# Strassen-Winograd MLP, mixers and experts on one core: a plain first block, one load of small parameters, another split of the convolutions' weights, and unread products

## The chip, the core and the metric

The kernel runs on one core of a Trainium2 chip. The core has five engines that follow their own instruction queues in order and wait for each other through semaphores: TensorE (PE in the profile; PEld is its weight load), VectorE (DVE), ScalarE (ACT), GpSimd (POOL) and SyncE (SP, which issues most DMA transfers). The metric is the device time of one execution in microseconds; of several runs the median counts, and less is better.

## The reference

One sequence of 512 tokens with 1024 features goes through two layers of a first kind and one of a second, all in float32. Cut to what matters here:

```python
# layers 0 and 1
p = x @ w_in[l]                                     # split into the mixers' inputs
y = concat(mla(...), mlstm(...), ssd(conv(s_xbc)))  # conv: 5 taps per channel, bias, silu
x = layernorm(alpha * x + y @ w_out[l])
x = layernorm(alpha * x + moe(x))                   # 4 groups of 4 experts, top 2, width 256
# third layer
x = x + mixer2(x) @ w_out_2                         # gated delta net and a linear recurrence
h = rmsnorm(x, norm_mlp_w_2) @ w_ff1_2              # 1024 -> 4096
x = rmsnorm(x + relu(h) ** 2 @ w_ff2_2, final_norm_w_2)
```

## The kernel before, in words

**Numbers.** A float32 operand of a product is held as a pair, h (rounded by a cast, L134) and l (the difference, L139); `split` makes both, with the engines that it is given, and `mm` (L124, L125, L126) adds three products, h·h, l·h and h·l. So each weight costs one cast and one subtraction of 128 x 1024 elements per half megabyte, and TensorE three passes.

**Weights.** `plan` lists all weights in the order of use as tasks; `take`, `done` and `pump` load them ahead (`load`, L229: a transfer of 1 MB from SP into one of two raw buffers, then the split into a ring of four). `self.pat` says which engine makes which half: ("act", "dve") at launch, ("act", "pool") after the gates' projection (L520). A raw buffer is free again when its splits are done.

**Order.** The program is written against a tile framework: each tile name has a number of buffers, and a new tile of a name waits for the readers of the old one. A list scheduler sets the order of every engine's instructions at build time from the dependencies and estimated times; the source does not fix it. Within a queue the order is then strict.

**Launch** (`run`, L1996). Four tiles of xT are loaded and split, `params` (L2007) loads nine small arrays for this and the next layer one by one into tiles of their own (L2014), and `mixer_layer` begins with the gates' projection "C", 312 columns for each of four token tiles, evacuated by `evac_c` (L507 to L515).

**Convolution** (`ssd_conv`, L580). For each of six feature blocks: ScalarE copies the projection into xp (L592), VectorE makes the first tap (L594) and four more (L596), ScalarE a tanh (L598), VectorE the product (L600); TensorE transposes four of the blocks (L605). Beside it stand the gates of the mLSTM (L703 to L725) and the next weights' splits.

**Routing** (`route`, before L1213; the mask sums at L1217 to L1220). From the logits LG a chain of small VectorE operations finds the group and the two best experts; `slot_ids` (L1128, L1141) makes the list of tokens for an expert, an indirect gather (L1089) fetches them, TensorE transposes them (L1096) and multiplies.

**Layer end** (`layer`). After the last expert eight indirect gathers (L2147) bring back the two results of each token into Yg, which are weighted and added (L2161, L2168), normalised, and transposed (L369, L371) for the next layer.

**MLP** (`second`, `mlp`). w_ff1_2 is used in eight blocks of 512 columns, w_ff2_2 in eight of 512 rows. The up product of a block, (512 x 1024) by (1024 x 512), is made as 2 x 2 blocks by Winograd's form of Strassen: seven products of half size (24 instructions each) instead of eight, for which VectorE forms four sums of weights (`up_part`, L260 to L264) and four sums of tokens T1 to T4 (`mlp_in`, L1779 to L1786, once). `fin(i)` ends token tile i of the third layer's mixer: the norm (L1333), eight transposes (L1770), copies into X32 (L1771) and splits. Two of block 0's products (B11, B21) are started early as `begun`. `keep` (L1806, L1807) combines the products, squares, and splits into uT; `down` adds the second product into R (L1837).

PSUM is given out by kind ("mm", "tr", "sm", "dn", "ht"), a few banks each.

Of the kernel before, what the change touches and what calls it, by code (L numbers as in the profile page):

```python
# [8 lines left out]
FR = mybir.dt.float32r  # L9
# [3 lines left out]
OP = mybir.AluOpType  # L13
AX = mybir.AxisListType

P = 128
# [54 lines left out]
class Kernel:  # L71
# [57 lines left out]

    def split(self, dst, src, heng="act", leng="dve"):  # L130

        nc = self.nc
        if heng == "act":
            nc.scalar.copy(dst.h, src)  # L134
        elif heng == "pool":
            nc.gpsimd.tensor_scalar(dst.h, src, 1.0, None, op0=OP.mult)
        else:
            nc.vector.tensor_copy(dst.h, src)
        (nc.gpsimd if leng == "pool" else nc.vector).tensor_tensor(dst.l, src, dst.h, op=OP.subtract)  # L139
# [104 lines left out]

    def up_part(self, b, n, u):

        v = self.nc.vector
        if n == 0:
            self.quarters = []
            for j in range(2):  # L250
                raw = self.t(self.raws[self.nraw % len(self.raws)].pool, "raw", [P, 2 * UNIT])
                self.nraw += 1
                at = b * 512 + j * 256
                self.nc.sync.dma_start(raw.rearrange("p (k n) -> p k n", n=256),
                                       self.a["w_ff1_2"][0][:, at:at + 256].rearrange("(k p) n -> p k n", p=P))
                self.quarters += [raw[:, 0:UNIT], raw[:, UNIT:2 * UNIT]]
# [229 lines left out]
    def mixer_layer(self, l):  # L486
# [33 lines left out]
        self.pat = [("act", "pool")]  # L520
# [25 lines left out]
        self.mla_in(l, m, sp, XT)  # L546
        yc = self.ssd_scan(l, sp, m, Z)
# [32 lines left out]
    def ssd_conv(self, l, m, XT):  # L580
# [7 lines left out]
        def evac(f, p):  # L588
# [5 lines left out]
            nc.vector.tensor_scalar(ac, xp[:, 0:S], cw[:, f:f + 1], cw[:, 30 + f:31 + f], op0=OP.mult, op1=OP.add)  # L594
# [567 lines left out]
    def route(self, pool, LG):  # L1162
# [17 lines left out]


# [4 lines left out]
        v.scalar_tensor_tensor(e2, o1, NEG, el, op0=OP.mult, op1=OP.add)  # L1186
        m2, o2 = top("o2", e2)
# [571 lines left out]
    def mlp_in(self, m, i, n, X, X32):  # L1759


        nc, v = self.nc, self.nc.vector
        tk, half = slice(i % 2 * P, i % 2 * P + P), i // 2
        cut = lambda n: HL(X[n].h[:, :, tk], X[n].l[:, :, tk])
        ps = []
        for g in range(2):
            p = self.ps("tr", [P, 4, P])
            for j in range(4):
                f = 4 * g + j
                nc.tensor.transpose(p[:, j, :], n[:, f * P:(f + 1) * P], self.ident)  # L1770
            nc.scalar.copy(X32[g][:, :, i * P:(i + 1) * P], p)  # L1771
            if not half:
                self.split(cut(("B11", "B21")[g]), p)
            ps.append(p)
        if not half:
            return
        (b11, b12), (b21, b22) = [[x[:, :, z + i % 2 * P:z + i % 2 * P + P] for z in (0, 256)] for x in X32]
        t2 = self.t(m, "u2", [P, S], bufs=2).rearrange("p (k t) -> p k t", k=4)
        v.tensor_tensor(b11, b12, b11, op=OP.subtract)  # L1779
        v.tensor_tensor(t2, b22, b11, op=OP.subtract)  # L1780
        self.split(cut("T2"), t2)
        self.split(cut("T1"), b11)
        v.tensor_tensor(b12, b22, b12, op=OP.subtract)
        self.split(cut("T3"), b12)
        self.split(cut("B22"), ps[1])
        v.tensor_tensor(b21, b21, t2, op=OP.subtract)  # L1786
        self.split(cut("T4"), b21)
# [6 lines left out]
    def mlp(self, m, X, R, begun, finish):  # L1794

        nc, v = self.nc, self.nc.vector
        uT = {}

        def up(b):
# [17 lines left out]
            A, C = (product(0, "B11"), product(1, "B21")) if b else begun  # L1817
# [25 lines left out]
        up(0)  # L1843
# [10 lines left out]
    def second(self):  # L1854
        nc, a, v = self.nc, self.a, self.nc.vector
        with ExitStack() as c:
# [17 lines left out]
            X, begun = {}, []  # L1874

            w0 = [self.hl(rp, t, [P, UNIT]) for t in ("T3", "T4")]
            for n in range(2):
                self.up_part(0, n, w0[n])
            for t in ("B11", "B21", "B22", "T1", "T2"):
                X[t] = self.hl(rp, t, [P, 4, 256])  # L1880
# [3 lines left out]
            def fin(i):  # L1884
                n = self.t(rp, "nrm", [P, D], bufs=2)
                if i == 2:
                    for z in range(2):
                        p = self.ps("dn", [P, S])
                        self.up_product(p, self.by_k(w0[z]), X[("B11", "B21")[z]])
                        begun.append(p)  # L1890
                    for t in ("T3", "T4"):
                        X[t] = self.hl(rp, t, [P, 4, 256])
                self.rms(rp, n, R[:, i], g, jk=n)
                self.mlp_in(rp, i, n, X, X32)
# [4 lines left out]
            with ExitStack() as x1:  # L1899
# [11 lines left out]
                self.mlp(rp, X, R, begun, finish)  # L1911

    def plan(self):
# [42 lines left out]
        def up(b):  # L1956
            for n in range(0 if b else 2, 7):
# [12 lines left out]
    def run(self):  # L1970
        nc, a = self.nc, self.a
        with ExitStack() as ctx:
# [13 lines left out]
            with ExitStack() as c2:  # L1986
                xp = self.pool(c2, "x0", bufs=4, side="right")
                self.tasks = self.plan()
                for i in range(NT):
                    xt = self.t(xp, "xt", [P, KD, P])  # L1990
                    nc.sync.dma_start(xt, a["xT"][i])
                    if i == 0:
                        self.consts()
                        self.set_phase("m", [self.raw0], [self.ring0], [("act", "dve")])
# [12 lines left out]
    def params(self, l):  # L2007

        self.par = r = {}
        width = dict(dtb=8, al=8, sgn=256, cw=48, gcol=32, lc=32, gc=16)  # L2010
        at = 0
        for tag, n in ROWS[l]:
            r[tag] = self.t(self.ppool, "gcol" if tag == "lc" else tag, [P, width.get(tag, n)])[:, 0:n]
            self.nc.sync.dma_start(r[tag], self.a[f"small{l}"][:, at:at + n])  # L2014
            at += n

# [9 lines left out]
    def layer(self, l):  # L2026
# [4 lines left out]
        with ExitStack() as c:  # L2031
# [72 lines left out]
            for s in range(16 + 4):  # L2104
# [10 lines left out]
                if s < 16:  # L2115
                    idx = self.slot_ids(mo, PM[:, s, :], 0, "idx")
                    ex[s] = self.expert(mo, [self.part((l, z, s)) for z in "gud"], idx, store(s))
# [31 lines left out]
            self.gate = [Yg[3][0]] * 2  # L2149
            for i in range(NT):  # L2150
# [92 lines left out]
```

## Time and profile before

| | us |
|---|---|
| median of three runs | 1737.26 |
| lowest and highest | 1736.63, 1739.16 |
| profiled execution | 1732.17 |
| its span | 1730.3 |

The profile is of one execution. Its times are in microseconds from the start of the span. An engine's busy time is the time in which it computes or moves data, without waits and without issuing transfers. In a timeline a row is an instruction (x2: two of the same kind in a row) with its start and duration, its engine, line, operation, and out<-in by the program's names; in brackets stand the idle time of the engine before it and what ended that. Durations of matmuls overlap, since they are pipelined: the distance from start to start is what one costs. PEclk is the granted clock of TensorE, as a share of full speed.

### The profile page before, as it was taken

How to read it: one execution, taken by the hardware profiler on the slowest of the kernel's cores; microseconds unless marked ns; L12 is line 12 of the kernel's file. 1: busy time of each engine (PE TensorE's matmuls, PEld its weight loads, DVE VectorE, ACT ScalarE, POOL GpSimd, SP SyncE). 2: the span in 40 equal slices, each digit the busy share in tenths (PEclk: the TensorE clock that was granted, in tenths of full speed). 3: DMA queues.
4: the chain of work that ended last, by engine and by line, in shares of the span. 5: the costliest groups of instructions: out<-in, count | busy, mean ns of one | idle time of the engine just before them, and what ended most of it. 6: DMA issues, size and time to landing. Idle time of an engine off the chain costs nothing. (4 is left out here: it accounts for less than half of the span.)

```text
span 1730.3 us, 29609 instructions
## 1 busy us (share of the span) xinstructions
PE 1561.6 (90%) x11539; PEld 1398.0 (81%) x11539; DVE 1298.5 (75%) x2480; ACT 827.2 (48%) x1422; POOL 561.3 (32%) x464
## 2 busy tenths in 40 slices
PE   7899999699956899997889993999799799999997
PEld 6789899698946789887878972887578698899996
DVE  6847963789957847865689977777776797777774
ACT  4354562278856344551368863555532533333331
POOL 0555332316114555334315202003411143444341
PEclk9999999899987999999989996999999899999999
DMA  5214123499945211123399964432112243333311
GB/s 183 61 59 147 64 103 115 180 363 357 396 166 204 61 59 48 50 86 131 127 346 358 373 239 170 128 98 74 38 52 75 73 127 117 98 98 98 98 62 49
DMA packets 107662, 248.02 MB, mean 143 GB/s; under 512 B 9460, under 2 KB 70776, under 8 KB 95224
## 3 DMA queue, kind: packets, MB, share of 16 engines
q1 hardware_dynamic: 101624, 225.05, 37.4%
q0 software_dynamic: 5888, 20.97, 3.8%
q8 instruction: 94, 1.54, 0.4%
q14 instruction: 56, 0.46, 0.1%
HBM read 218.21 MB, written 27.79 MB: 142 GB/s over the span
## 5 line engine op out<-in xcount | busy, mean ns | idle before, releaser
L134 ACT CAST wh<-raw 128x1024 fp32r<-128x1024 f32 (+3 forms) x375 | 377.5, 1024 | 278.4 <-PE mm L126 70.3
L139 POOL TENSOR_TENSOR wl<-raw,wh 128x1024 fp32r<-128x1024 f32 (+3 forms) x117 | 281.3, 2414 | 474.7 <-ACT wh L134 469.0
L139 DVE TENSOR_TENSOR wl<-raw,wh 128x1024 fp32r<-128x1024 f32 (+2 forms) x258 | 307.2, 1211 | 64.3 <-ACT wh L134 63.4
L124 PE MATMUL mm<-wh,actTh 128*128 128x256 f32 (+2 forms) x640 | 189.5, 297 | 22.2 <-ACT wh L134 7.9
L126 PE MATMUL mm<-wh,actTl 128*128 128x256 f32 (+2 forms) x640 | 185.7, 292 | 2.9 <-POOL actTl L139 2.4
L125 PE MATMUL mm<-wl,actTh 128*128 128x256 f32 (+2 forms) x640 | 185.9, 291 | 0.5 <-DVE wl L139 0.5
L124 PE MATMUL mm<-actTh,wh 128*128 128x512 f32 x368 | 150.5, 409 | 2.4 <-DVE FD L509 0.8
L126 PE MATMUL mm<-actTh,wl 128*128 128x512 f32 x368 | 148.0, 402 | 0.0
L125 PE MATMUL mm<-actTl,wh 128*128 128x512 f32 x368 | 148.0, 402 | 0.0
L124 PEld LDWEIGHTS mm<-wh,actTh 128*128 128x128 f32 x640 | 124.9, 195 | 25.2 <-ACT wh L134 7.9
L126 PEld LDWEIGHTS mm<-wh,actTl 128*128 128x128 f32 x640 | 123.9, 194 | 5.4 <-POOL actTl L139 3.3
L125 PEld LDWEIGHTS mm<-wl,actTh 128*128 128x128 f32 x640 | 124.8, 195 | 1.8 <-DVE wl L139 0.9
L1089 POOL DMA_INDIRECT G<-Xd,idx x32 | 77.9, 2434 | 131.1 <-DVE oh L1138 58.3
L124 PE MATMUL dn<-wh,uTh 128*128 128x512 f32 x256 | 100.9, 395 | 3.1 <-DVE R L1837 3.1
L126 PE MATMUL dn<-wh,uTl 128*128 128x512 f32 x256 | 100.4, 392 | 0.0
L125 PE MATMUL dn<-wl,uTh 128*128 128x512 f32 x256 | 100.1, 391 | 0.1
L124 PEld LDWEIGHTS mm<-actTh,wh 128*128 128x128 f32 x368 | 70.6, 192 | 17.8 <-PE mm L126 2.2
L126 PEld LDWEIGHTS mm<-actTh,wl 128*128 128x128 f32 x368 | 70.9, 193 | 14.4
L125 PEld LDWEIGHTS mm<-actTl,wh 128*128 128x128 f32 x368 | 71.0, 193 | 14.0
L124 PE MATMUL py<-wh,GTh 128*96 128x256 f32 x256 | 73.6, 287 | 1.3 <-ACT wh L134 1.3
L124 PE MATMUL pg<-wh,GTh 128*96 128x256 f32 x256 | 74.3, 290 | 0.0
L125 PE MATMUL py<-wl,GTh 128*96 128x256 f32 x256 | 72.9, 285 | 1.1 <-DVE wl L139 1.1
(781 smaller groups left out, 4308.4 us busy)
## 6 DMA issues: line engine op xcount, KB each, us to landing
raw<-in_expert_w_gate_dram SPq DMA_DIRECT2D x32, 1024.0 KB, 10.4
raw<-in_expert_w_up_dram SPq DMA_DIRECT2D x32, 1024.0 KB, 10.3
raw<-in_expert_w_down_dram SPq DMA_DIRECT2D x32, 1024.0 KB, 10.9
raw<-in_w_ff_dram SPq DMA_DIRECT2D x32, 1024.0 KB, 5.5
raw<-in_w_in_dram SPq DMA_DIRECT2D x27, 1024.0 KB, 5.4
raw<-in_w_out_dram SPq DMA_DIRECT2D x12, 1024.0 KB, 5.2
Yd<-Ye SPq DMA_DIRECT2D x32, 384.0 KB, 6.7
Yd<-zr SPq DMA_DIRECT2D x9, 512.0 KB, 6.4
```

What stands on the lines that cost most here:

```text
L124: mm(out, lhsT.h, rhs.h, start=start, stop=False, **kw)
L125: mm(out, lhsT.h, rhs.l, start=False, stop=False, **kw)
L126: mm(out, lhsT.l, rhs.h, start=False, stop=stop, **kw)
L134: nc.scalar.copy(dst.h, src)
L139: (nc.gpsimd if leng == "pool" else nc.vector).tensor_tensor(dst.l, src, dst.h, op=OP.subtract)
L1089: nc.gpsimd.indirect_dma_start(out=G[:n], out_offset=None, in_=self.Xd, in_offset=bass.IndirectOffsetOnAxis(ap=idx[:n], axis=0))
```

## The change

- `busy(kind, x, n)` is new: n float32 products of a matrix of ones with x into a tile of PSUM that nobody reads. It is called at launch after the constants (14 times, with the ones themselves), in `route` on LG (10) and on e2 (8), after `slot_ids` for the first four experts (4 on LG), and at the layer end on the first 128 columns of each of the eight gathered tiles (3 each).
- `params` makes one tile "par" and one transfer per layer. The tags are slices of it.
- In `ssd_conv` the first tap moves from VectorE to ScalarE (activation Identity with scale and bias). `self.pat` becomes ("act", "pool") only after the convolutions and the inputs of the attention, so the weights of that stretch get both halves from ScalarE and VectorE.
- MLP: block 0 is a plain product (`up_plain`), 192 instructions, with its four weight tiles as they are (`up_block0`, loaded and split before). It runs feature half by feature half within each token half: (f, t) = (0, 0), (1, 0), (0, 1), (1, 1). The token sums move from `mlp_in` to `mlp_sums`, behind the first quarter of block 0's products, and are taken over 256 tokens at a time; their splits go into the memory of block 0's weights: T2 and T1 after the third quarter, T3 and T4 after the fourth. B12, which the seven products do not need, is held in a raw buffer. Results are relu, square and split, without sums.

```diff
@@ -126,6 +126,12 @@
...
             self.nc.tensor.matmul(out, lhsT, rhs, start=start, stop=stop, **kw)
+    def busy(self, kind, x, n):
+        p = self.ps(kind, [P, x.shape[1]])
+        for _ in range(n):
+            self.nc.tensor.matmul(p, self.ones, x, start=True, stop=True)
@@ -242,18 +248,27 @@
...
+    def up_load(self, b):
+        q = []
+        for j in range(2):
+            raw = self.t(self.raws[self.nraw % len(self.raws)].pool, "raw", [P, 2 * UNIT])
+            self.nraw += 1
+            at = b * 512 + j * 256
+            self.nc.sync.dma_start(raw.rearrange("p (k n) -> p k n", n=256),
+                                   self.a["w_ff1_2"][0][:, at:at + 256].rearrange("(k p) n -> p k n", p=P))
+            q += [raw[:, 0:UNIT], raw[:, UNIT:2 * UNIT]]
+        return q
+    def up_block0(self, ws):
+        for n, (q, w) in enumerate(zip(self.up_load(0), ws)):
+            self.split(w, q, "act", ("dve", "pool")[n // 2])
     def up_part(self, b, n, u):
...
         if n == 0:
-            self.quarters = []
-            for j in range(2):
-                raw = self.t(self.raws[self.nraw % len(self.raws)].pool, "raw", [P, 2 * UNIT])
-                self.nraw += 1
-                at = b * 512 + j * 256
-                self.nc.sync.dma_start(raw.rearrange("p (k n) -> p k n", n=256),
-                                       self.a["w_ff1_2"][0][:, at:at + 256].rearrange("(k p) n -> p k n", p=P))
-                self.quarters += [raw[:, 0:UNIT], raw[:, UNIT:2 * UNIT]]
+            self.quarters = self.up_load(b)
         q = self.quarters
         if n == 2:
             q.append(self.t(self.mlpp, "sw", [P, UNIT]))
@@ -517,7 +532,6 @@
...
         self.cT = self.hl(m, "cT", [P, 3, S])
-        self.pat = [("act", "pool")]
@@ -544,6 +558,7 @@
...
         self.mla_in(l, m, sp, XT)
+        self.pat = [("act", "pool")]
         yc = self.ssd_scan(l, sp, m, Z)
         self.sctx.close()
         with ExitStack() as y:
@@ -591,7 +606,7 @@
...
             ac = self.t(m, "ac", [P, S], bufs=2)
-            nc.vector.tensor_scalar(ac, xp[:, 0:S], cw[:, f:f + 1], cw[:, 30 + f:31 + f], op0=OP.mult, op1=OP.add)
+            nc.scalar.activation(ac, xp[:, 0:S], AF.Identity, scale=cw[:, f:f + 1], bias=cw[:, 30 + f:31 + f])
             for k in range(1, 5):
                 nc.vector.scalar_tensor_tensor(ac, xp[:, k:k + S], cw[:, 6 * k + f:6 * k + f + 1], ac, op0=OP.mult, op1=OP.add)
             th = self.t(m, "th", [P, S])
@@ -1178,12 +1193,14 @@
...
+        self.busy("ht", LG.rearrange("p t e -> p (t e)"), 10)
...
         v.scalar_tensor_tensor(e2, o1, NEG, el, op0=OP.mult, op1=OP.add)
+        self.busy("ht", e2.rearrange("p n e -> p (n e)"), 8)
         m2, o2 = top("o2", e2)
         gl = LG[:, :, 0:4]
         gm, og = top("og", gl)
@@ -1756,45 +1773,64 @@
...
-    def mlp_in(self, m, i, n, X, X32):
-        nc, v = self.nc, self.nc.vector
+    def mlp_in(self, i, n, X, X32):
+        nc = self.nc
         tk, half = slice(i % 2 * P, i % 2 * P + P), i // 2
-        cut = lambda n: HL(X[n].h[:, :, tk], X[n].l[:, :, tk])
-        ps = []
         for g in range(2):
             p = self.ps("tr", [P, 4, P])
             for j in range(4):
                 f = 4 * g + j
                 nc.tensor.transpose(p[:, j, :], n[:, f * P:(f + 1) * P], self.ident)
+            x = X[f"B{g + 1}{half + 1}"]
+            self.split(HL(x.h[:, :, tk], x.l[:, :, tk]), p)
             nc.scalar.copy(X32[g][:, :, i * P:(i + 1) * P], p)
-            if not half:
-                self.split(cut(("B11", "B21")[g]), p)
-            ps.append(p)
-        if not half:
-            return
-        (b11, b12), (b21, b22) = [[x[:, :, z + i % 2 * P:z + i % 2 * P + P] for z in (0, 256)] for x in X32]
-        t2 = self.t(m, "u2", [P, S], bufs=2).rearrange("p (k t) -> p k t", k=4)
+    def mlp_sums(self, X, X32):
+        v = self.nc.vector
+        (b11, b12), (b21, b22) = [[x[:, :, z:z + 256] for z in (0, 256)] for x in X32]
         v.tensor_tensor(b11, b12, b11, op=OP.subtract)
-        v.tensor_tensor(t2, b22, b11, op=OP.subtract)
-        self.split(cut("T2"), t2)
-        self.split(cut("T1"), b11)
         v.tensor_tensor(b12, b22, b12, op=OP.subtract)
-        self.split(cut("T3"), b12)
-        self.split(cut("B22"), ps[1])
-        v.tensor_tensor(b21, b21, t2, op=OP.subtract)
-        self.split(cut("T4"), b21)
+        v.tensor_tensor(b22, b22, b11, op=OP.subtract)
+        v.tensor_tensor(b21, b21, b22, op=OP.subtract)
+        return dict(T1=b11, T2=b22, T3=b12, T4=b21)
...
-    def mlp(self, m, X, R, begun, finish):
+    def mlp(self, m, X, X32, w0, R, finish):
...
         uT = {}
+        def up_plain():
+            u_ = self.hl(m, "uT", [P, 4, S], bufs=2)
+            W = [self.by_k(w) for w in w0]
+            C, T = [], {}
+            for f, t in ((0, 0), (1, 0), (0, 1), (1, 1)):
+                p = self.ps("dn", [P, S])
+                for z in range(2):
+                    for k in range(KD):
+                        x = X[f"B{k // 4 + 1}{t + 1}"][:, k % 4]
+                        self.mm(p[:, z * 256:(z + 1) * 256], W[2 * f + k // 4][k % 4][:, z * P:(z + 1) * P], x,
+                                start=k == 0, stop=k == KD - 1)
+                C.append((f, t, p))
+                if (f, t) == (0, 0):
+                    T = self.mlp_sums(X, X32)
+                for n in {(0, 1): ("T2", "T1"), (1, 1): ("T3", "T4")}.get((f, t), ()):
+                    X[n] = self.hl(m, n, [P, 4, 256])
+                    self.split(X[n], T[n])
+            for f, t, p in C:
+                r, u = self.t(m, "nrm", [P, D], bufs=2)[:, 0:S], self.t(m, "u2", [P, S], bufs=2)
+                nc.scalar.activation(r, p, AF.Relu)
+                v.tensor_tensor(u, r, r, op=OP.mult)
+                self.split(HL(*(x[:, 2 * f:2 * f + 2, 256 * t:256 * t + 256] for x in (u_.h, u_.l))),
+                           u.rearrange("p (f t) -> p f t", f=2), "act")
+            uT[0] = u_
@@ -1814,7 +1850,7 @@
...
-            A, C = (product(0, "B11"), product(1, "B21")) if b else begun
+            A, C = product(0, "B11"), product(1, "B21")
             nc.scalar.copy(s1, A)
             keep(0, 0, s1, C)
             v.tensor_tensor(s1, s1, product(2, "T2"), op=OP.add)
@@ -1840,7 +1876,7 @@
...
-        up(0)
+        up_plain()
         for b in range(8):
             if b < 7:
                 up(b + 1)
@@ -1871,27 +1907,20 @@
...
             self.bcast_load(g, a["norm_mlp_w_2"][0], D)
-            X, begun = {}, []
-            w0 = [self.hl(rp, t, [P, UNIT]) for t in ("T3", "T4")]
-            for n in range(2):
-                self.up_part(0, n, w0[n])
-            for t in ("B11", "B21", "B22", "T1", "T2"):
-                X[t] = self.hl(rp, t, [P, 4, 256])
+            w0 = [self.hl(rp, t, [P, UNIT]) for t in ("T2", "T1", "T3", "T4")]
+            self.up_block0(w0)
+            X = {t: self.hl(rp, t, [P, 4, 256]) for t in ("B11", "B21", "B22")}
+            b12 = self.t(self.raw0.pool, "raw", [P, 2 * UNIT]).bitcast(FR).rearrange("p (z k t) -> p z k t", z=2, k=4)
+            X["B12"] = HL(b12[:, 0], b12[:, 1])
             X32 = self.hl(rp, "uT", [P, 4, S], bufs=2)
             X32 = [x.bitcast(F32) for x in (X32.h, X32.l)]
...
                 n = self.t(rp, "nrm", [P, D], bufs=2)
-                if i == 2:
-                    for z in range(2):
-                        p = self.ps("dn", [P, S])
-                        self.up_product(p, self.by_k(w0[z]), X[("B11", "B21")[z]])
-                        begun.append(p)
-                    for t in ("T3", "T4"):
-                        X[t] = self.hl(rp, t, [P, 4, 256])
                 self.rms(rp, n, R[:, i], g, jk=n)
-                self.mlp_in(rp, i, n, X, X32)
+                self.mlp_in(i, n, X, X32)
                 self.dump("x3", R[:, i], i)
@@ -1908,7 +1937,7 @@
...
-                self.mlp(rp, X, R, begun, finish)
+                self.mlp(rp, X, X32, w0, R, finish)
@@ -1954,7 +1983,7 @@
...
         def up(b):
-            for n in range(0 if b else 2, 7):
+            for n in range(7 if b else 0):
                 add(("up", b, n), "p", [], 4, 256)
                 T[-1].make = lambda u, n=n: self.up_part(b, n, u)
@@ -1991,6 +2020,7 @@
...
                         self.consts()
+                        self.busy("sm", self.ones, 14)
                         self.set_phase("m", [self.raw0], [self.ring0], [("act", "dve")])
                     self.split(self.actT[:, :, i * P:(i + 1) * P], xt)
             self.params(0)
@@ -2007,12 +2037,12 @@
...
         self.par = r = {}
-        width = dict(dtb=8, al=8, sgn=256, cw=48, gcol=32, lc=32, gc=16)
+        all_ = self.t(self.ppool, "par", [P, max(sum(n for _, n in z) for z in ROWS)])
         at = 0
         for tag, n in ROWS[l]:
-            r[tag] = self.t(self.ppool, "gcol" if tag == "lc" else tag, [P, width.get(tag, n)])[:, 0:n]
-            self.nc.sync.dma_start(r[tag], self.a[f"small{l}"][:, at:at + n])
+            r[tag] = all_[:, at:at + n]
             at += n
+        self.nc.sync.dma_start(all_[:, 0:at], self.a[f"small{l}"])
@@ -2114,6 +2144,8 @@
...
                     idx = self.slot_ids(mo, PM[:, s, :], 0, "idx")
+                    if s < 4:
+                        self.busy("ht", LG.rearrange("p t e -> p (t e)"), 4)
                     ex[s] = self.expert(mo, [self.part((l, z, s)) for z in "gud"], idx, store(s))
                     next(ex[s])
                 for z in (1, 2, 3):
@@ -2147,6 +2179,9 @@
...
             self.gate = [Yg[3][0]] * 2
+            for i in range(NT):
+                for j in range(2):
+                    self.busy("ht", Yg[i][j][:, 0:P], 3)
             for i in range(NT):
                 r = R[:, i]
                 if l == 0 or i < 2:
```

## Rows read from the trace of the kernel before

**Rows 1.** The page, part 1: busy us, share of the span, instructions.
```profile
PE 1561.6 (90%) x11539; PEld 1398.0 (81%) x11539; DVE 1298.5 (75%) x2480; ACT 827.2 (48%) x1422; POOL 561.3 (32%) x464
```

**Rows 2.** Windows: stretch; busy PE, PEld, DVE, ACT, POOL; PEclk, DMA, GB/s.
```profile
60.00:80.00 20.00, 16.55 (x62) 13.14 (x63) 17.08 (x32) 7.49 (x13) 11.87 (x15) 0.83 0.34 105
1060.00:1080.00 20.00, 13.74 (x43) 8.69 (x41) 19.61 (x76) 9.61 (x21) 0.00 (x0) 0.79 0.30 118
1370.00:1380.00 10.00, 1.24 (x6) 0.91 (x6) 10.00 (x15) 6.88 (x11) 0.00 (x0) 0.61 0.00 0
1380.00:1400.00 20.00, 17.26 (x114) 16.15 (x115) 19.90 (x22) 8.41 (x12) 5.16 (x1) 0.77 0.35 107
```

**Rows 3.** Timelines at launch: start, duration, engine, line, operation, [idle before <-releaser].
```profile
9.07 0.63 PE L125 MATMUL mm<-wl,actTh 128*128 128x312 f32 x1 [0.54 <-DVE wl L139]
...
13.66 0.36 PE L125 MATMUL mm<-wl,actTh 128*128 128x312 f32 x1
...
17.85 0.31 PE L126 MATMUL mm<-wh,actTl 128*128 128x312 f32 x1
20.61 0.63 PE L124 MATMUL mm<-wh,actTh 128*128 128x312 f32 x1 [2.45 <-DVE Yc L515]
...
17.92 1.04 ACT L134 CAST wh<-raw 128x1024 fp32r<-128x1024 f32 x1 [4.98 <-DMA raw<-in_w_in_dram]
...
12.70 1.01 SPq L229 DMA_DIRECT2D raw<-in_w_in_dram  x2
```

**Rows 4.** Groups by line (28 to 84); timelines and a wait, both convolutions.
```profile
L596 DVE SCALAR_TENSOR_TENSOR ac<-xp,cw,ac 128x512 f32<-128x512 f32 x22 | 20.0, 908 | 0.4
L594 DVE TENSOR_SCALAR ac<-xp,cw 128x512 f32<-128x512 f32 x6 | 8.0, 1329 | 4.1 <-ACT xp L592 4.1
L139 DVE TENSOR_TENSOR wl<-raw,wh 128x1024 fp32r<-128x1024 f32 x3 | 3.7, 1222 | 0.3 <-ACT wh L134 0.3
...
42.28 0.74 DVE L596 SCALAR_TENSOR_TENSOR ac<-xp,cw,ac 128x512 f32<-128x512 f32 x1
...
45.14 4.04 DVE L594 TENSOR_SCALAR ac<-xp,cw 128x512 f32<-128x512 f32 x1 [0.45 <-ACT xp L592]
...
44.71 2.38 POOL L139 TENSOR_TENSOR wl<-raw,wh 128x1024 fp32r<-128x1024 f32 x1 [1.07 <-ACT wh L134]
...
PE tr L605 <- DVE BC L600: 2.9, 1, 2.9
...
594.28 1.09 PE L605 MATMUL tr<-ident,BC 128*128 128x128 f32 x4 [3.58 <-DVE MP L725]
```

**Rows 5.** Timeline of TensorE at layer 0's routing.
```profile
336.14 0.17 PE L1218 MATMUL sm<-Mb,triS 128*128 128x16 bf16 x1 [7.63 <-DVE Mb L1213]
...
343.56 1.54 PE L1096 MATMUL tr<-ident,G 96*128 96x96 f32 x8 [2.90 <-DMA G<-Xd,idx]
...
347.94 0.42 PE L124 MATMUL pg<-wh,GTh 128*96 128x256 f32 x1
```

**Rows 6.** Timeline of TensorE at the end of layer 0.
```profile
530.33 1.97 PE L369 MATMUL tr<-ident,GTl 128*128 128x128 f32 x8 [26.06 <-ACT GTl L2168]
```

**Rows 7.** Timeline of TensorE in the MLP's first blocks.
```profile
1360.37 0.28 PE L124 MATMUL dn<-B11h,T3h 128*128 128x256 f32 x1
...
1379.41 0.58 PE L124 MATMUL tr<-T1h,wh 128*128 128x256 f32 x1 [7.86 <-ACT wh L134]
...
1397.80 0.28 PE L124 MATMUL mm<-T4h,wh 128*128 128x256 f32 x1
...
1400.62 0.28 PE L124 MATMUL mm<-B11h,wh 128*128 128x256 f32 x1
...
1435.19 0.51 PE L124 MATMUL dn<-wh,uTh 128*128 128x512 f32 x1 [3.14 <-DVE R L1837]
```

**Rows 8.** Timeline of SP: small loads.
```profile
43.55 0.33 SPq L2014 DMA_DIRECT2D al<-in_small_dram  x1
...
210.49 0.34 SPq L2014 DMA_DIRECT2D mng<-in_small_dram  x1
```

## The prediction

> **What bounds the kernel now.** I read the page first: TensorE is busy 1561.6 us of the 1730.3 us span, so all its waits together are worth at most 169 us [rows 1]. The page's 40 slices show where they sit, and I read windows over those places, for two numbers: idle time and granted clock. A clock near 0.5 is the lower of two levels (1.2 GHz), 1.00 the upper (2.4 GHz). Where TensorE is always busy, 20 us at a mean of 0.77 have lost 20 x 0.23 = 4.6 us of work [rows 2]. Last come the timelines and the waits, for what ended each idle stretch:
>
> - Launch: products of 312 columns stand 0.27 us apart (17 steps from 9.07 to 13.66), then 0.144 (29 steps to 17.85). After 2.45 us of idle the clock is low again: the product at 20.61 takes 0.63. ScalarE had stood 4.98 us behind a weight load that SP issued only at 12.70, after the small parameter loads, and what empties the products' banks stood behind it [rows 3].
> - Convolutions: VectorE sets the pace, and GpSimd holds it up. A first tap takes 4.04 us beside a GpSimd subtraction of 2.38 and more GpSimd work after it; the mean of the six is 1.33. TensorE then waits 2.9 us, in layer 1 3.58 [rows 4].
> - Routing: 7.63 us idle on VectorE's chain, then 2.90 for the first gather, then slow products from 343.6 to beyond 347.9 [rows 5]. Layer 1 repeats it.
> - Layer ends: 26.06 us idle behind indirect gathers, and transposes at the low clock after it [rows 6].
> - First MLP block: it runs from 1360.4 to 1400.6. TensorE has 7.86 us idle while VectorE forms weight and token sums one after the other (10.00 of 10 us busy), and then the low clock [rows 2, 7].
>
> **The change part by part.** All sums stand against the profiled execution, 1732.17 us, whose span is 1730.3; it lies 5.09 us under the median of the runs, 1737.26, and I add that at the end.
>
> **First MLP block.** It drops the four weight sums, the token sums ahead of the first products and the combinations of quadrants, and makes 192 products instead of 168. 24 products take 2.82 us (1397.80 to 1400.62), 0.1175 each, so 192 take 22.6 [rows 7]. Half of them (11.3 us) need tokens 0 to 255 and plain weights alone, which are there when the last projection ends at 1360.4. Tile 3, which the other half needs, had its transposes done when TensorE fell idle at 1379.41 - 7.86 = 1371.5, so its halves come in time. With 1.5 us for these transposes in between, the block ends at 1360.4 + 22.6 + 1.5 = 1384.5, 16.1 us before 1400.6.
>
> Next late is VectorE. By 1385 it has eight half-tile splits (half of 1.22 each, 4.9), four token sums of full width and four splits of them (8 x 1.22 = 9.8), four results (4 x 2 x 0.61 = 4.9), and of block 1 three weight sums and three splits (7.3) [rows 4]: 27 us for some 25. The splits of T3 and T4 must moreover wait until the plain weights in the same memory are read. So block 1 may stand 1 to 3 us; I take 2. The 3.14 us wait at 1435.19, for an addition into R that VectorE is late with, may go with the lighter start; I take half of it or 1.6, less 1.7 because block 1's two weight loads now land just ahead of their use [rows 7]. Taken: 16.1 - 2 + 1.6 - 1.7 = 14. Ends: 8, if VectorE sets the pace and half is lost, and 16.1 + 3.1 = 19. B12 keeps a raw buffer until the block's last product; the load that goes there next is used 20 us later, so this costs nothing, and up to 5 us if that load is late (a load lands in 5.2 us: issued 12.70, ScalarE released 17.92) [rows 3].
>
> **Launch.** The 14 unread products are 28 instructions; eight slow ones of 128 columns take 1.97 us [rows 6], so 28 x 0.25 = 7 us from about 1 us, when the constants are there, to 8. They fill the time before the first product and delay it by 0.1 at most. If the clock is up by then, 17 steps at 0.27 become 0.144: 2.1 us. SP issues one small load instead of nine, so the weight load goes out when its buffers come free, one to two us earlier: I take 1.5 of the 2.45 us idle, and the slow stretch behind it, about twelve steps, gives 1.5. Sum 5.1; ends 0 (the products don't count for the clock, the loads are bound by the buffers) and 2.1 + 2.45 + 1.5 = 6.1 [rows 3]. In layer 1 and the third layer the single load must wait for the last reader of the old tile. The last small loads of today that wait so are issued at 210.49 [rows 8], hundreds of us before the next layer: hidden, if it is issued there.
>
> **Convolutions.** Off VectorE: the six first taps (8.0 us), and in the 22 other taps what lies above the 0.74 of an undisturbed one (20.0 - 16.3 = 3.7). On it: six weight halves at 1.22, 7.3 [rows 4]. With the small instructions caught in the same way (I count some 5 us) the net is 9 us. ScalarE gains 6 x 0.6 and is half idle. But TensorE waits less than this: 2.9, and in the window 60 to 80 a clock of 0.83 costs up to 20 x 0.17 = 3.4 [rows 2, 4]. The launch's gain must also come through this stage, which VectorE bounds. I take 3.4 for layer 0, 8.5 with the launch; ends 3 and 13. Layer 1 has the 3.58 us idle and a slow stretch after it (four transposes at 1.09): 4.5 taken, ends 0 and 7 [rows 4].
>
> **Routing.** Ten products of 80 columns and eight of 64 stand in TensorE's in-order queue inside its idle 7.63 us: 36 instructions at less than 0.25, under 7; four more follow each slot. If they hold the clock over the gather, the slow stretch 343.6 to 348 gives half its time, 2.2, in each layer; I take 2.5 of 4.4. Ends 0.5 lost (the fourth slot's products share a bank with the first expert's transposes) and 4.4 [rows 5].
>
> **Layer ends.** 24 products of 128 columns wait for the eight gathers. At the first end they can lift the clock for the eight transposes at 530.33 (half of 1.97) and the products behind them, which I estimate at routing's 2.2: at most some 3 us [rows 5, 6]. At the second VectorE is busy 19.61 of 20 us right after the gathers, so nothing [rows 2]; and products for a late gather hold up the first sums in the queue, up to 2. I take 1, ends -2 (a loss) and 3.
>
> Sum: 14 + 8.5 + 4.5 + 2.5 + 1 = 30.5. Profiled 1732.2 - 30.5 = 1701.7, and with 5.1 on it **1707 us**.
>
> **The rivals.** *VectorE stays the bound.* For it: 10.00 of 10 us where the MLP starts, and the weight halves leave GpSimd for the busier engine [rows 2, 4]. Then the MLP gives 8, launch and layer 0 together 4, layer 1's convolution 0, the rest 3: 15 us, 1722. Against it: what the MLP drops on VectorE (four weight sums, four combinations) is more than what it adds.
>
> *The unread products do not hold the clock.* For it: at 20.61 the clock was low after only 2.45 us idle, and between the last slot and the transposes 2.90 remain [rows 3, 5]. Then 2.1 + 2.5 + 1 go: 25 us, 1712.
>
> After the transposes at 343.56 the experts' products still ran slow for four us [rows 5]. The Trainium skill (TensorE: Matmul & The Clock Gate, Part 4: PE-mode transpose) says that a transpose does not count as busy time for the clock in the way a product does; this row agrees. By that the transposes don't bridge from the slots' unread products to the experts, and routing gives 0: this same rival.
>
> *Slower: SP's queue.* The one parameter load waits for its tile, and SP issues in order. If it is placed where the first of the small loads stands now, at 43.55, every weight load behind it waits until 210 [rows 8], and attention and mLSTM have no weights: 100 us or more, in two layers, 1840 at the least. It decides whether the issue stands ahead of a weight load that is needed before its tile is free. Against it: each of today's small loads stands behind its own last reader, so the schedule follows the readers.
>
> *It doesn't do what it says:* the new block waits for its weights or VectorE as long as the old, and the other stages shift by as much to either side: 1735.
>
> **How the numbers follow.** Forecast (1697 to 1716): 0.56. VectorE: 0.18. No clock: 0.16. No effect: 0.06. SP's queue, or a loss through the new order: 0.04. The upper end of the range takes in the VectorE case with 2 us on it; the lower end is short of all better bounds at once (19 + 13 + 7 + 4.4 + 3 = 46, 1691): 1692 to 1724. About 0.2%, 3.5 us, is what a measurement of this kernel can tell from no change. Faster: 0.56 + 0.18 + 0.16 = 0.90; within: 0.06; slower: 0.04.
>
> **What would show it.** MLP: the first product of block 1 near 1385 on the scale of before, no idle over 2 us up to there. Launch: products 0.14 apart from the first on, no 2.45 us idle, the weight load before 12. Convolutions: no tap over 1 us, weight halves on VectorE, the waits of 2.9 and 3.58 gone. Routing and ends: a granted clock near 1.00. The prediction is wrong if the taps get short and TensorE's waits stay, if a parameter load stands in SP's queue with a weight load behind it, or if block 0 ends early and block 1 then waits as long.

## The result, and the profile after

| | us |
|---|---|
| before, median of four runs | 1737.93 (1736.63 to 1739.16) |
| changed kernel, median of four runs | 1720.46 (1717.09 to 1721.76) |
| ratio | 0.9897, interval 0.9879 to 0.9914 |
| profiled execution of the changed kernel, its span | 1721.76, 1720.0 |

The change saves 17.5 us by the medians. The forecast was 1707, 30 us faster, with a range of 1692 to 1724. Two lines of the changed kernel's page, busy time and the clock in 40 slices:

```profile
PE 1613.3 (94%) x11823; PEld 1443.6 (84%) x11823; DVE 1272.9 (74%) x2466; ACT 839.1 (49%) x1433; POOL 519.3 (30%) x446
...
PEclk9999999799988999998979997999998999999999
```

TensorE's busy time grew by 52 us against [rows 1], while the span shrank: part of it is work that nobody reads, and not all of it was free.

Launch, timelines of TensorE and SP:

```profile
1.05 5.37 PE L134 MATMUL sm<-ones 128*128 128x128 f32 x28 [1.05 <-DVE ones L309]
7.62 0.41 PE L124 MATMUL mm<-wh,actTh 128*128 128x312 f32 x1 [1.20 <-ACT wh L140]
8.79 0.63 PE L125 MATMUL mm<-wl,actTh 128*128 128x312 f32 x1 [0.76 <-DVE wl L145]
...
12.08 0.31 PE L126 MATMUL mm<-wh,actTl 128*128 128x312 f32 x1
...
18.02 0.41 PE L124 MATMUL mm<-wh,actTh 128*128 128x312 f32 x1 [0.73 <-DVE Yc L530]
...
9.81 2.23 SPq L235 DMA_DIRECT2D raw<-in_w_in_dram  x2
```

The 28 instructions of the unread products (L134 is the product in `busy`) end before 7. The first product of 312 columns behind them takes 0.41 us, the next, after two waits of 1.20 and 0.76 us, 0.63: the clock was up and fell back. The products are fast from 12.08 instead of 13.66, the weight load leaves at 9.81 instead of 12.70, and of the 2.45 us idle 0.73 are left [rows 3].

Convolution of layer 0, groups by line, and a window:

```profile
L611 DVE SCALAR_TENSOR_TENSOR ac<-xp,par,ac 128x512 f32<-128x512 f32 x24 | 18.7, 785 | 1.0 <-ACT ac L609 0.8
L145 DVE TENSOR_TENSOR wl<-raw,wh 128x1024 fp32r<-128x1024 f32 x10 | 12.5, 1262 | 5.1 <-ACT wh L140 5.1
...
L609 ACT ACTIVATE ac<-xp,par 128x512 f32<-128x512 f32 x6 | 4.9, 809 | 0.6 <-DVE UR L722 0.4
...
60.00:80.00 20.00, 20.00 (x94) 16.03 (x92) 15.29 (x29) 9.48 (x16) 7.83 (x7) 1.00 0.33 106
```

L611 is the old L596: 785 ns in the mean instead of 908; the longest of the 48 in both layers takes 1.10 us. The first tap stands on ScalarE at 809 ns, the lower weight halves (L145, the old L139) on VectorE. TensorE is busy 20.00 of 20 us at clock 1.00 where it had 16.55 and 0.83 [rows 2, 4]; neither convolution has a wait of TensorE left.

Routing of layer 0, timelines of VectorE and TensorE, and a window:

```profile
314.88 1.96 PE L2112 MATMUL sm<-rw,Ye 128*128 128x20 f32 x16 [0.71 <-ACT Ye L2106]
...
319.39 0.24 DVE L2113 SCALAR_TENSOR_TENSOR LG<-sm,lnrs,rb 128x20 f32<-128x20 f32 x1
...
324.16 0.22 DVE L1230 TENSOR_TENSOR Mb<-M,M 128x64 bf16<-128x64 f32 x1
...
319.68 4.56 PE L134 MATMUL ht<-LG,ones 128*128 128x80 f32 x20 [2.84 <-DVE LG L2113]
324.30 3.67 PE L134 MATMUL ht<-e,ones 128*128 128x64 f32 x16
327.77 0.22 PE L1235 MATMUL sm<-Mb,triS 128*128 128x16 bf16 x1
...
335.08 1.54 PE L1111 MATMUL tr<-ident,G 96*128 96x96 f32 x8 [0.51 <-DMA G<-Xd,idx]
...
342.91 0.40 PE L125 MATMUL pg<-wl,GTh 128*96 128x256 f32 x1
...
343.26 0.28 PE L124 MATMUL pg<-wh,GTh 128*96 128x256 f32 x1
...
320.00:340.00 20.00, 19.26 (x113) 18.64 (x112) 12.55 (x64) 1.86 (x5) 4.94 (x8) 0.50 0.59 204
```

The first row is the logit products. Mb, the mask of the chosen experts, is ready at 324.4, but the mask sums that need it (L1235, the old L1218) start at 327.77: the 36 unread instructions stand ahead of them, 4.56 and 3.67 us long. The clock stays at 0.50 all the while, and the experts' products get fast only at 343.3.

End of layer 0, TensorE, and windows:

```profile
500.05 0.39 PE L126 MATMUL mm<-wh,hTl 128*96 128x512 f32 x1
515.48 1.62 PE L134 MATMUL ht<-GTl,ones 128*128 128x128 f32 x6 [15.04 <-DMA GTl<-Yd,row]
518.10 1.62 PE L134 MATMUL ht<-GTl,ones 128*128 128x128 f32 x6 [1.00 <-DMA GTl<-Yd,row]
519.78 5.75 PE L134 MATMUL ht<-G,ones 128*128 128x128 f32 x24
525.58 1.93 PE L134 MATMUL ht<-raw,ones 128*128 128x128 f32 x12
528.37 1.09 PE L384 MATMUL tr<-ident,GTl 128*128 128x128 f32 x8 [0.86 <-ACT GTl L2203]
...
516.00:523.00 7.00, 5.88 (x24) 4.87 (x22) 5.38 (x11) 1.68 (x3) 4.08 (x4) 0.50 0.97 360
525.00:530.00 5.00, 3.48 (x25) 2.68 (x23) 2.67 (x9) 2.48 (x3) 3.76 (x10) 1.00 0.18 75
531.00:537.00 6.00, 5.16 (x20) 4.74 (x21) 2.19 (x11) 4.93 (x8) 2.86 (x4) 0.50 0.43 175
```

L134 is again the unread products, 48 instructions in four rows, between the experts' last product and the transposes of the rows handed to layer 1 (L384); TensorE waits 0.86 us more behind them. The clock does rise behind these products: the eight transposes take 1.09 us instead of 1.97 [rows 6]. But at the next layer's first products, from 531, it is low again.

The MLP, windows (busy time of PE, PEld, DVE, ACT, POOL, then the clock) and all waits of TensorE from 1360 to 1445:

```profile
1360.00:1380.00 20.00, 20.00 (x172) 19.96 (x172) 15.38 (x32) 11.63 (x20) 2.50 (x1) 1.00 0.48 159
1380.00:1400.00 20.00, 20.00 (x168) 19.93 (x167) 19.97 (x20) 12.66 (x17) 3.10 (x2) 1.00 0.50 159
...
PE dn L125 <- POOL wl L145: 1.7, 1, 1.7
PE dn L124 <- DVE R L1873: 1.1, 1, 1.1
```

The waits are 1.7 us for a weight half from GpSimd and 1.1 us for an addition into R. TensorE is at 20.00 of 20 us and clock 1.00 where it had stood 7.86 us [rows 2, 7].

The same stages of several kernels, worked out from the starts of TensorE's rows, in us. "To logits" is the span's start to the last logit products of layer 0; "experts" from there to the last h·h product of the last expert; "end" from there to the next layer's first product with 512 columns; "conv 1" from that to the first row sums of the mLSTM in layer 1; "mixer 3" from layer 1's end to the last h·h projection of the third mixer; "MLP" from there to the last product.

| kernel | to logits | experts 0 | end 0 | conv 1 | experts 1 | end 1 | mixer 3 | MLP |
|---|---|---|---|---|---|---|---|---|
| before | 326.5 | 176.9 | 49.7 | 59.3 | 180.4 | 61.7 | 260.9 | 360.6 |
| changed | 314.9 | 184.7 | 53.6 | 54.1 | 184.5 | 61.3 | 266.1 | 345.6 |
| no_route | 314.8 | 178.1 | 51.5 | 54.1 | 180.4 | 63.1 | 265.9 | 345.8 |
| no_slots | 313.3 | 181.3 | 53.5 | 54.1 | 183.3 | 62.1 | 265.9 | 345.5 |
| no_end | 314.7 | 187.3 | 49.8 | 54.1 | 186.0 | 64.5 | 263.4 | 345.8 |
| no_launch | 315.9 | 182.6 | 52.8 | 54.1 | 184.8 | 65.5 | 265.6 | 345.2 |
| no_busy | 316.8 | 178.6 | 49.8 | 54.1 | 179.2 | 61.0 | 263.7 | 345.5 |
| launch_busy | 313.8 | 177.7 | 49.3 | 54.1 | 179.6 | 63.1 | 265.6 | 346.8 |
| no_par | 320.9 | 178.2 | 49.1 | 53.3 | 180.8 | 60.7 | 260.8 | 346.2 |
| par_only | 323.4 | 177.8 | 49.0 | 60.9 | 178.1 | 61.8 | 265.6 | 361.1 |

The runs are named for what they leave out of the changed kernel, or for the one part that they put into the kernel before; the next section has them. One caution: mixer 3 is touched by no part of the change but the small loads, and single profiles of it differ by 5 us. The profiled execution of before (1732.17) lay below all four timed runs beside it; so the profiles stand 10.4 us apart and the medians 17.5.

### The profile page after: what moved, and what is told of

Its sections match the earlier page's. It is cut to its first block, busy times and chain, and to the rows that moved or that the text cites. A ratio compares the mean times of both kernels' runs of the same rounds, so it can differ in the third digit from the quotient of the medians.

```text
span 1720.0 us, 30113 instructions
## 1 busy us (share of the span) xinstructions
PE 1613.3 (94%) x11823; PEld 1443.6 (84%) x11823; DVE 1272.9 (74%) x2466; ACT 839.1 (49%) x1433; POOL 519.3 (30%) x446
## 5 line engine op out<-in xcount | busy, mean ns | idle before, releaser
L140 ACT CAST wh<-raw 128x1024 fp32r<-128x1024 f32 (+3 forms) x371 | 373.1, 1023 | 267.6 <-PE mm L126 67.3
L145 DVE TENSOR_TENSOR wl<-raw,wh 128x1024 fp32r<-128x1024 f32 (+1 forms) x273 | 328.4, 1223 | 79.4 <-ACT wh L140 77.5
L145 POOL TENSOR_TENSOR wl<-raw,wh 128x1024 fp32r<-128x1024 f32 (+2 forms) x98 | 230.9, 2366 | 377.1 <-ACT wh L140 371.6
L125 PE MATMUL pg<-wl,GTh 128*96 128x256 f32 x256 | 74.0, 289 | 0.1
```

The costliest lines, as they stand in the source:

```text
L125: mm(out, lhsT.h, rhs.l, start=False, stop=False, **kw)
```

## The experiments

All ratios are against runs of the kernel before on the same chip; times are medians.

**The unread products, taken away by place** from the changed kernel. no_route:

```diff
-        self.busy("ht", LG.rearrange("p t e -> p (t e)"), 10)
...
-        self.busy("ht", e2.rearrange("p n e -> p (n e)"), 8)
...
-                    if s < 4:
-                        self.busy("ht", LG.rearrange("p t e -> p (t e)"), 4)
```

Expected: 

> The changed kernel without the unread products at routing (the 10, the 8 and the 4 after each of four slots). Theory 'queue': they wait for LG and e2, run one behind the other at the low clock (4.56 and 3.67 us in the trace of after) and push the mask sums 3.3 us behind Mb in each layer, and the clock rises no earlier for them. Then 2 x 3.3 us come back, and 1 to 3 more from the slots: 1711 (1708 to 1714) against 1720.5. Rival 'clock', the step of the prediction: they save 2.5 us in all, and the mask sums are late for another reason; then 1723. A third: the schedule hides both, 1720 within 2.

Measured 1711.72, ratio 0.985 (0.9831 to 0.9869): 8 to 9 us come back. TensorE at routing, and a window:

```profile
324.38 0.17 PE L1233 MATMUL sm<-Mb,triS 128*128 128x16 bf16 x1 [7.21 <-DVE Mb L1228]
...
331.50 1.54 PE L1111 MATMUL tr<-ident,G 96*128 96x96 f32 x8 [2.59 <-DMA G<-Xd,idx]
...
336.55 0.37 PE L126 MATMUL pg<-wh,GTl 128*96 128x256 f32 x1
336.75 0.28 PE L124 MATMUL pg<-wh,GTh 128*96 128x256 f32 x1
...
320.00:340.00 20.00, 10.63 (x89) 10.33 (x89) 15.22 (x70) 4.23 (x8) 7.71 (x11) 0.58 0.84 286
```

The mask sums start as soon as Mb is there. "Clock" is refuted: 8 to 9 us come back where it has 2.5 lost. That the clock rises later for the unread products is not shown. From the first transposes to the fast products it takes 5.2 us here and 8.2 in the changed kernel (335.08 to 343.26), but 4.6 in no_end, which has them, and 7.7 in launch_busy, which hasn't; over both layers of all kernels it is 4.5 to 8.5 us with them and 4.2 to 7.9 without. What the traces show is that the products do not bring the rise forward.

no_slots takes the products after the slots away and leaves the others:

```diff
-                    if s < 4:
-                        self.busy("ht", LG.rearrange("p t e -> p (t e)"), 4)
```

Expected: 

> The changed kernel without the four unread products after each of the first four slots; those on LG and e2 stay. Theory 'queue': of the 8.7 us that all routing products cost, 6.6 hang on LG and e2, ahead of the mask sums, and 2 on the slots: 1718 (1716 to 1720). Rival: the slots delay the first experts, and most hangs on them: 1714 or less.

Measured 1715.42, ratio 0.9872 (0.985 to 0.9894), just below the band of "queue". TensorE:

```profile
326.18 0.22 PE L1235 MATMUL sm<-Mb,triS 128*128 128x16 bf16 x1
...
333.33 1.54 PE L1111 MATMUL tr<-ident,G 96*128 96x96 f32 x8 [2.65 <-DMA G<-Xd,idx]
...
341.53 0.41 PE L126 MATMUL pg<-wh,GTl 128*96 128x256 f32 x1
...
341.90 0.28 PE L125 MATMUL pg<-wl,GTh 128*96 128x256 f32 x1
```

The delay of the mask sums is still there: from the last logit products to them it takes 12.9 us in both layers of every kernel that has the products on LG and e2, and 9.5 to 9.6 in all others. So 3.3 us in each layer hang on these. By the medians the slots' share is 5.0 us and that of LG and e2 3.7; by the delay of the mask sums it is 2.1 and 6.6. The run does not decide between the two, and where the slots' products cost time is not shown: the first transposes come 7.2 us behind the mask sums here and 7.3 in the changed kernel.

no_end:

```diff
-            for i in range(NT):
-                for j in range(2):
-                    self.busy("ht", Yg[i][j][:, 0:P], 3)
```

Expected: 

> The changed kernel without the unread products at the two layer ends (8 times 3 in each). Theory 'queue': at the end of layer 0 the lead of 3.8 us with which the experts end is gone when the next layer's convolutions begin; if the products are its cause, 2 to 4 us come back: 1718 (1716 to 1720). Rival 'clock' (the prediction): they save 1 us, so without them 1721.5. Rival 'VectorE and GpSimd': the layer end is set by the normalisation chain, and the products matter to nobody: 1720.5 within 1.5.

Measured 1720.15, ratio 0.9894 (0.9877 to 0.9912): no difference. But end 0 takes 49.0 to 50.2 in all ten kernels without these products and 51.5 to 53.6 in the four with them; in no_end other stages, "experts 0" (187.3) above all, were longer in its one profile. That end 0 pays 2 to 4 us is shown by the traces; that the total moves by it is not.

no_launch:

```diff
-                        self.busy("sm", self.ones, 14)
```

Expected: 

> The changed kernel without the 14 unread products at launch. In the trace of after the products of the first projection get fast at 12.08, in that of before at 13.66. Theory: only these 1.6 us hang on them, and some of it is lost in the VectorE-bound convolution: 1721.5 (1720 to 1723). Rival, the prediction's price: 2.1 us, and the wait at 18 grows again: 1723 or more. Rival 'the clock comes up by itself': 1720.5 within 1.

Measured 1725.46, ratio 0.9931 (0.9915 to 0.9947), 5 to 6 us slower than the changed kernel, as the rival with the prediction's price has it. TensorE's first product:

```profile
7.66 0.63 PE L124 MATMUL mm<-wh,actTh 128*128 128x312 f32 x1 [7.66 <-ACT wh L140]
```

It takes 0.63 us, as at the low clock [rows 3], where the changed kernel has 0.41. But by the trace only 1.1 us of the 5 stand before the logits. End 1 took 65.5 instead of 61.3, with the transposes in another order; no_busy has this same order and 61.0, so the order alone doesn't explain it.

no_busy has the edits of no_route, no_end and no_launch together. Expected: 

> The changed kernel without any unread product. If the three places add up as the theories say: -9 at routing, -2 at the ends, +1 at launch: 1710.5 (1706 to 1714). By the prediction's prices (2.1 + 2.5 + 1 saved) it would be slower than the changed kernel: 1726.

Measured 1706.35, ratio 0.9838 (0.9818 to 0.9859). Together the unread products cost 14 us by the medians and 10 by the ratios. The single removals (-8.7, -0.3, +5.0) add up to -4, by the ratios to -3. Each ratio is known to about 3 us and the gap of 7 to 10 us is made of five of them, so it stands at the edge of the noise.

launch_busy has those of no_route and no_end. Expected: 

> The changed kernel with unread products at launch only (none at routing and layer ends). By the traces of the kernels with and without them, 1.2 to 1.9 us hang on them up to the end of the first convolution: 1704.5 (1702 to 1707) against 1706.4 without any. By the sum of the single removals (-8.7 and -0.3 from 1720.5) it would be 1711.5; then the order at the layer ends, not the products, makes the difference.

Measured 1707.37, ratio 0.9835 (0.9818 to 0.9852), as without any. So the 5 us of no_launch are not the worth of the launch products: in the trace of launch_busy they bring the logits 3.0 us forward against no_busy, and the total does not keep it. What costs no_launch its 5 us stays open.

**The parts alone, on the kernel before.** mlp_only, the plain block with all that belongs to it (as in the diff above, without the rest):

```diff
-        up(0)
+        up_plain()
...
-                self.mlp_in(rp, i, n, X, X32)
+                self.mlp_in(i, n, X, X32)
```

Expected: 

> The kernel before with the plain first MLP block alone. Theory (the prediction's term, 14, and the 16 us that the traces show between the last projection of the mixer and the MLP's later blocks): 1722 (1720 to 1724). Rival 'VectorE stays the bound' : 8 us, 1729.

Measured 1719.45, ratio 0.9911 (0.9893 to 0.9929), 15 to 18 us; from the last projection to the end its trace has 346.4 instead of 360.6. The rival is refuted: VectorE does not take half of the gain.

tap_only:

```diff
-            nc.vector.tensor_scalar(ac, xp[:, 0:S], ...)
+            nc.scalar.activation(ac, xp[:, 0:S], AF.Identity, ...)
```

pat_only:

```diff
-        self.pat = [("act", "pool")]
...
         self.mla_in(l, m, sp, XT)
+        self.pat = [("act", "pool")]
```

conv_only has both. Expected: 

> The kernel before with the first tap on ScalarE and both halves of the weights split on ScalarE and VectorE during convolutions and the attention's inputs, alone. Theory: without GpSimd's subtractions VectorE no longer bounds the convolutions; 5 us in layer 1 as the trace of after shows and 6 to 7 in layer 0: 1726 (1723 to 1729). The prediction's terms (3.4 and 4.5) give 1729. Rival 'VectorE stays the bound': the weight halves eat the gain, 4 us or less, 1733 or more.

Measured 1722.84, ratio 0.9919 (0.9902 to 0.9935): 14 us, more than any of the three gave as its middle; "VectorE stays the bound" falls. By the trace layer 0 gains 6.3 us up to the logits (320.2 instead of 326.5) and layer 1's convolution 6.0 (53.3 instead of 59.3).

tap_only, expected: 

> The kernel before with the first tap of the convolutions on ScalarE alone; GpSimd still makes the lower weight halves. Theory 'GpSimd': what held VectorE up were GpSimd's subtractions, and the tap is only 0.55 us each: 3 us of the 14.3 that both parts give, 1734 (1732 to 1737). Rival 'tap': the tap is the instruction that is caught worst (1.33 us mean, 4.04 at most), and moving it takes most: 1727 or less.

Measured 1727.25, ratio 0.9951 (0.9934 to 0.9969): 8.5 us by the ratio, where theory "GpSimd" had 3. Groups by line, layer 0:

```profile
L139 POOL TENSOR_TENSOR wl<-raw,wh 128x1024 fp32r<-128x1024 f32 x8 | 20.3, 2538 | 48.1 <-ACT wh L134 46.3 <-PE tr L605 1.8
...
L596 DVE SCALAR_TENSOR_TENSOR ac<-xp,cw,ac 128x512 f32<-128x512 f32 x24 | 22.0, 919 | 0.4
```

pat_only, expected: 

> The kernel before with the weights of the convolutions and of the attention's inputs split on ScalarE and VectorE, the first tap left on VectorE. Theory 'GpSimd': 10 us of the 14.3, 1727 (1724 to 1730). Rival 'tap': less than 5, 1733 or more.

Measured 1720.52, ratio 0.9904 (0.9883 to 0.9924): 17 us, more than either of the two gave. Groups by line, layer 0:

```profile
L596 DVE SCALAR_TENSOR_TENSOR ac<-xp,cw,ac 128x512 f32<-128x512 f32 x24 | 19.2, 799 | 0.5
L139 DVE TENSOR_TENSOR wl<-raw,wh 128x1024 fp32r<-128x1024 f32 x11 | 13.4, 1220 | 1.8 <-ACT wh L134 1.4 <-issue 0.3
L594 DVE TENSOR_SCALAR ac<-xp,cw 128x512 f32<-128x512 f32 x6 | 4.3, 713 | 0.8 <-ACT xp L592 0.8
```

With the tap away GpSimd still makes eight halves, and the other taps still take 919 ns; VectorE has only lost the 8.0 us of its first taps. With the halves away, all taps are short (799 and 713 ns) and VectorE has eight more subtractions of 1.22. So it is GpSimd's subtractions that stretch the taps. In both runs the wait of 2.9 us for VectorE [rows 4] is gone from TensorE; either edit does that, and the two do not add up: 8.5 and 17 alone, 14 together. The tap on top of the halves brings nothing that can be measured.

par_only, expected: 

> The kernel before with the one load of small parameters alone. Theory (the prediction): the weight load leaves SP at about 10 to 11 instead of 12.7 and the wait at 18 shrinks: 3 us, 1734 (1732 to 1736). Rival 'buffers': the raw buffers bind the load, or the VectorE-bound convolution swallows the gain: 1737 within 1.5. Slower by more than 3: a parameter load stands in SP's queue ahead of weights.

```diff
-            self.nc.sync.dma_start(r[tag], self.a[f"small{l}"][:, at:at + n])
+        self.nc.sync.dma_start(all_[:, 0:at], self.a[f"small{l}"])
```

Measured 1737.26, ratio 1.0001 (0.9988 to 1.0014): nothing, as rival "buffers" has it, though not by its reason, since the weight load leaves at 10.17 and the logits come 3.1 us earlier. no_par is no_busy with the loads of before:

```diff
-            r[tag] = all_[:, at:at + n]
+            self.nc.sync.dma_start(r[tag], self.a[f"small{l}"][:, at:at + n])
```

Expected: 

> The plain block and the convolutions' parts without any unread product, and with the small loads one by one as before. If the one load is worth its 4 us of the trace (launch and first convolution) once VectorE no longer bounds them: 1710 (1708 to 1712) against 1706.4. Rival: it is worth nothing, as alone: 1706.5 within 1.5.

Measured 1706.19, ratio 0.9825 (0.9803 to 0.9846), as no_busy. The 3 to 4 us before the logits are there in both pairs of traces (326.5 and 323.4, 320.9 and 316.8), and in both pairs mixer 3 was longer with the one load (260.9 and 265.6, 260.8 and 263.7). Over all traces mixer 3 takes 263.4 to 266.1 us in the eight kernels with the one load and 260.8 to 264.8 in the six without: the one load seems to lose there what it gains at launch. Why stays open. no_par, the plain block and the convolutions' parts alone, is faster than the changed kernel by 12 to 14 us and than the kernel before by 31.

## Why the prediction was right in direction and 13 us too low

The time lies in the stated range, but outside the forecast's own 1697 to 1716, and 1.5 us from the 1722 of the rival "VectorE stays the bound". That rival's mechanism is refuted in both places, so landing there is chance: 31 us gained, 10 to 14 thrown away.

- **MLP.** Forecast 14, measured 15.0 between the last projection and the end, 15.5 by the ratio of mlp_only. The step held: products of tokens 0 to 255 fill the wait. Of the waits that the sum feared, the 2 us of block 1 did not come: the scheduler put its first products between block 0's last ones from 1377 on, and TensorE is busy without a gap up to 1400. The other two came as 1.7 us for weights at 1404 and 1.1 for R at 1423, instead of 3.1 before.
- **Launch and layer 0's convolution.** Forecast 8.5, by the traces 11.6 up to the logits. The direction held, the split didn't: over half is the convolution (6.3 in conv_only), and of the 3 to 4 us that the one load gives up to the logits nothing is found in the total.
- **Layer 1's convolution.** Forecast 4.5, measured 5.2.
- The term that was mis-sized in these two is the convolutions': 3.4 + 4.5 forecast, 14 measured alone. The rows had it nearly right: the wait of 2.9 and the slow stretch of 3.4 [rows 2, 4] are together the 6.3 that layer 0 gains in conv_only. I halved them for fear that VectorE would keep the rest, and it keeps nothing once GpSimd is out of its way.
- **Routing.** Forecast 2.5 saved, measured 8 to 9 lost. The failed step is "under 7 us inside the idle 7.63", and both of its numbers fail. 36 instructions at nearly 0.25 are up to 9 us, not under 7; they took 0.23 each, 8.1 together. And the wait begins 7.63 us before 336.14, at 328.5 [rows 5], but the products need LG, and VectorE's timeline of the kernel before has it only at 331.3:

```profile
331.09 0.24 DVE L2083 SCALAR_TENSOR_TENSOR LG<-sm,lnrs,rb 128x20 f32<-128x20 f32 x1
...
335.86 0.22 DVE L1213 TENSOR_TENSOR Mb<-M,M 128x64 bf16<-128x64 f32 x1
```

  So 4.8 us were free for 8.1 us of queued work; the rest, 3.3, is the measured delay. The clock's share, 2.2 us in each layer, did not come: no trace has an earlier rise for these products.
- **Layer ends.** Forecast 1 saved, with 2 to lose by the queue; by the traces end 0 loses 2 to 4, and at end 1 nothing is found. The clock was up for the eight transposes, as forecast (0.9 us), but not for the products behind them.
- **The rivals.** "The unread products do not hold the clock" (25 us) is right at routing, and in part elsewhere, but gave them no cost of their own. What came out is no_par's 31 us, from the MLP and the convolutions, less the 10 to 14 that the unread products took. "SP's queue" fell: the single loads for the later layers were issued at 197.8 and 730.7, after the last reader of the old tile, VectorE's L858. "VectorE" fell in both places.

## What to carry to other kernels

Filler work in an in-order queue is free only between the moment its own operand is ready and the moment the next real operand is: measure that gap, not the engine's idle time, which begins earlier. Where two edits relieve one engine, try each alone: the second may be worth nothing once another engine sets the pace. And before the parts of a build-time schedule are added up, leave each out, and all of them: single removals here were -8.7, -0.3 and +5.0, and the removal of all three -14.

## What was not expected of the hardware

- TensorE was busy 19.26 of 20 us in the window 320 to 340 of the changed kernel, with the unread products, the slots and the first transposes, and the granted clock stood at 0.50, the lower level. (Without the products it was busy 10.63 and the mean was 0.58, because the rise at 336.7 falls into that window.) At end 0 the clock did rise behind the unread products, from 0.50 in 516 to 523 to 1.00 in 525 to 530, and fell again. The Trainium skill (TensorE: Matmul & The Clock Gate, Part 1: The HAM clock gate) says that the slow clock is the default and activity releases it. End 0 agrees; at routing the profile shows a busy engine and no release, and there the measurement decides. What sets the two apart no run here shows.
- At launch 14 unread products did raise the clock, but it did not always hold: the first product of 312 columns took 0.41 us in all five kernels with them and 0.63 in all nine without. In launch_busy and no_slots the products were then fast throughout, in the other three only from 11.9 to 12.5; in the nine without them from 12.1 to 15.4. The wait behind the unread products was longer in launch_busy (2.26 us) than in the changed kernel (1.20), so the wait alone does not decide it.
